# A three-branch decoder layer on eight cores: projection blocks in another order, and side branches whose waits are prepared further ahead

## The chip, the cores and the metric

The kernel runs on all 8 cores of one Trainium2 chip, and each core computes one element of the batch (2,048 tokens). The time is the device time of the slowest core in microseconds (us). Lower is better. Cores 0 to 3 are one die, cores 4 to 7 the other.

Most executions of one kernel agree within 1.5%. Some fall into a second, slower state in which the cores of one die, sometimes of both, show a lower granted TensorE clock; most of these take 6 to 14% longer, with a mean clock of 0.77 to 0.88 on a die, where the cores of fast runs have 0.89 to 0.97; a few take only up to 4% longer. Such runs are marked slow. A median, where one is given, is of all runs of that kernel, slow ones too.

Engines as the profile names them: PE is TensorE (matmuls), PEld its weight load, DVE is VectorE, ACT is ScalarE, POOL is GpSimd, SP is SyncE, which here only issues DMA transfers. `L289` is a line of the kernel file. L289 is the one helper that issues every matmul, so groups are told apart by their tiles.

## The reference, cut to what matters

```python
h = rms_norm(x, norm[l])
proj = h @ w_in[l]                                  # (B,S,IN_DIM)
(m_qk, m_v, m_o, m_z, m_i, m_f, a_cq, a_ckv, a_kr, a_z, c_q, c_z, gates) = split_cols(proj)
# A: mLSTM
qk = jax.nn.silu(causal_depthwise_conv(m_qk, conv_w[l], conv_b[l]))      # 4 taps
...
hm = mlstm_chunkwise(mq, mk, mv, ig, lf)
hm = rms_norm(hm, ...) * jax.nn.sigmoid(m_o) * jax.nn.silu(m_z)
# B: latent attention, 8 heads, causal softmax
...
ha = causal_block_attention(qa, ka, v_a) * jax.nn.silu(a_z)
# C: 4 heads over 256 memory tokens
hc = memory_attention(c_q, mkv[:, :, 0], mkv[:, :, 1]) * jax.nn.silu(c_z)
# merge
merged = g_m * (hm @ w_br_m[l]) + g_a * (ha @ w_br_a[l]) + g_c * (hc @ w_br_c[l])
x = x + merged @ w_out[l]
return rms_norm(x, final_norm)
```

## The kernel before

All instructions are written out by Python generators. A dense generator (projections, later the merge) always has TensorE work. A side generator (latent attention, then mLSTM, then memory attention) has long chains of waits. A scheduler alternates them: each `yield` tells how much TensorE time was just written, and the side generator gets a share of the dense one's.

```python
def dense_all():
    yield from p0_gen()      # norm of x, latent projections
    yield from p1_gen()      # latent up-projections, rotary
    yield from p2_gen()      # conv q/k blocks, values, output gates
    yield from p3_gen()      # memory queries and gates: cq0 cz0 cq1 cz1
    yield from d_gen()       # gates, merge, output

sides = [(mla_gen, "MLA", 0.36), (mlstm_gen, "ML", 0.36), (c_gen, "CC", 0.36)]
```

In the timelines looked at here an engine's instructions come in the order in which they were written (SyncE's in the changed kernel, 1,880 to 1,920 us: `cq`, `cz`, the store of the sums, two stores of `hc`, `rbc`, the same in every step). This matters throughout: an instruction that is ready still stands behind one that waits (in b1 below TensorE waits 56.7 us for loads that are written behind another load, in b5, where they are written ahead of it, 3.1 us).

One conv block is 16 matmuls into one bank and then this:

```python
copy("act", p[:, 3:515], bk[:, 0:512], [r_bk], [], accs=[p.r])
ts("dve", y[:], p[:, 3:515], cw[:, j, 3:4], cb[:, j:j + 1], ALU.mult, ALU.add, [p.r, r_k], [y.r])
for tap in (2, 1, 0):
    stt(y[:], p[:, tap:tap + 512], cw[:, j, tap:tap + 1], y[:], ALU.mult, ALU.add, [p.r, y.r, r_k], [y.r])
act(th[:], y[:], AF.Tanh, [y.r], [th.r], scale=0.5)
stt(o[:], th[:], 1.0, y[:], ALU.add, ALU.mult, [th.r, y.r], [o.r])
```

The mLSTM works in 16 chunks of 128 tokens. `mb` is a broadcast of the cumulative decay from device memory to all 128 partitions, `Cf` the state (f32), `Cb` its bf16 copy.

```python
B2s = tiles("mb", 2, [128, 4, 128], F32, top=True)
...
def loads1(c):                 # values, output gates, decay
    ...
    fw.dma("sp", B2s[c % 2][:], BHv[:, cols].partition_broadcast(128), reads=[dr("BH")], writes=[B2s[c % 2].r])

def P1a(c):                    # exponentials, scores, transposed keys
    act(EB[:], B2[:], AF.Exp, [B2.r], [EB.r])
    tt("dve", BM[:], B2[:], Mneg[:]..., ALU.add, [B2.r, Mneg.r], [BM.r])
    ...                        # q*EB on Pool, q.k matmuls, exp per head, product, transposes
def P1b(c, h):                 # state update of one head
    for kc in range(2):
        bu, r_bu = bub.next()                       # two banks in turn
        mm(bu, r_bu, ..., kw[:, h, kc * 128:(kc + 1) * 128], v2[:, h, 0:257], True, True, [kw.r, v2.r])
        stt(Cf[:, h, kc, 0:257], Cf[:, h, kc, 0:257], EB[:, h, 127:128], bu[:, 0:257], ALU.mult, ALU.add, ...)
    copy("act", Cb[:, h, :, 0:257], Cf[:, h, :, 0:257], [Cf.rs[h]], [Cb.rs[h]])
def P2(c, hp):                 # output of two heads, then their norm on VectorE
    ...
    rsqrt(sc[:, 8:10], sc[:, 6:8], sc[:, 10:12], sc.r)          # 14 steps on 128x2 numbers
    for e_ in range(2):
        stt(ht[:], bo[:, 0:256], sc[:, 8 + e_:9 + e_], g2[...], ALU.mult, ALU.mult, ...)

for c in range(16):
    if c + 1 < 16:
        P1a(c + 1)
    if c < 15:
        for h in range(4):
            P1b(c, h)
    hl = P2(c, 0); hl += P2(c, 1)
    if prev is not None:
        tail(c - 1, prev)
    prev = hl
    loads1(c + 2)              # the decay of chunk c+2 is asked for here
```

Memory attention runs in 16 steps (4 heads x 4 query blocks). The inverse of the softmax sums is a row of 512 numbers that must be in all 128 partitions. It goes to device memory (`RDC`) and comes back as a broadcast (`rbc`):

```python
for si, (h, qb) in enumerate(steps):
    ps = nxt
    if si + 2 < 16:
        loads(si + 2)                                  # cq, cz, three buffers each
    if si + 1 < 16:
        nxt = scores(si + 1)
    ...                                                # 8 narrow matmuls: the sums
    fw.op("dve", lambda e: e.reciprocal(out=rd[:], in_=dn[:, 0:4]), ...)
    fw.op("pe", lambda e: e.transpose(out=dn[0:4, 128:256], in_=rd[:], identity=identf[:]), ...)
    copy("dve", rt_[:], dn[0:4, 128:256], [r_dn], [rt_.r])
    fw.dma("sp", RDC_d[...], rt_[:], ...)
    fw.dma("sp", rb[:], RDC_d[h:h + 1, cols].partition_broadcast(128), ...)
    ...                                                # P.V matmuls, u = out * cz
    if fin[0] is not None:
        fin[0]()                                       # the step before: hc = u * rb, store HCT
    fin[0] = fin_
```

The softmax here doesn't subtract the row's maximum and nothing guards it: scores larger than these inputs give would overflow.

## Time and profile before

The kernel took 3,651.69 us (median of three runs, 3,631.66 to 3,657.26). The profiled execution has a span of 3,699.6 us on its slowest core, core 6. That is more than the timed runs took: in this execution cores 6 and 7 stayed some 75 us longer in the mLSTM than the other six cores, whose spans are 3,597 to 3,625 us. The page of that execution: busy time of each engine with its share of the span, then the span in 40 slices of 92.5 us, each digit the busy share of a slice in tenths (PEclk: the granted clock in tenths of full speed).

```profile
span 3699.6 us, 41439 instructions; the slowest of 8 cores (3597.0 to 3699.6 us)
...
PE 2875.4 (78%) x13618; PEld 1367.3 (37%) x13885; DVE 1295.0 (35%) x2738; ACT 761.1 (21%) x1509; POOL 341.2 (9%) x410
...
PE   3679569877779999944444446748999999999998
...
PEclk9889789989899999977777678969999999999999
```

TensorE is the busiest engine by far. Where its digits are 9 it has next to no idle time; where they are 3 to 7 it waits for something else, and that is the time a change can win. The next view gives the busy time of each engine (and the count of instructions) in five stretches of core 6, then the granted clock, the share of the DMA engines and GB/s. The stretches are: x phase and latent projections; projections with latent attention beside them; mLSTM; memory attention; merge and output.

```profile
0.00:524.00 524.00, 335.89 (x1738) 168.67 (x1768) 184.97 (x247) 158.84 (x326) 34.64 (x41) 0.86 0.45 117
524.00:1590.00 1066.00, 916.98 (x4454) 458.24 (x4541) 597.46 (x1236) 284.82 (x562) 6.87 (x13) 0.94 0.30 73
1590.00:2290.00 700.00, 311.92 (x1458) 148.89 (x1487) 243.15 (x875) 137.70 (x320) 35.79 (x32) 0.71 0.24 51
2330.00:2524.00 194.00, 116.42 (x537) 49.26 (x546) 53.11 (x102) 27.19 (x47) 11.49 (x19) 0.74 0.67 156
2524.00:3699.00 1175.00, 1154.37 (x5253) 524.20 (x5358) 208.31 (x267) 145.98 (x243) 252.41 (x306) 0.99 0.51 101
```

The mLSTM stretch is the worst: 312 of 700 us busy, at a clock of 0.71. The chain of waits inside one of its chunks (start, length, what; the line "issue" is time in which the engine waited for nothing that the profile shows) says why:

```profile
1860.98 16.63 DMA mb_122_13302<-BH
1877.71 0.70 DVE BM_127_13307 L302
1878.50 0.41 ACT DT_128_13308 L293
...
1882.80 0.49 DVE Cf_13317 L309
1883.42 4.02 PE bk L289 x10
```

The decay load is issued when the chunk before it is done, takes 16.63 us, and only then do the exponentials, the product and the state updates run, one after the other. What TensorE waited for in the mLSTM stretch (tile and engine that released it: us in total, times, longest) has the same cause in its first line, because the state update `Cf` stands behind the load:

```profile
PE bk L289 <- DVE Cf_13317 L309: 280.7, 57, 23.5
```

### The profile page before, as it was taken

How to read it: one execution, taken by the hardware profiler on the slowest of the kernel's cores; microseconds unless marked ns; L12 is line 12 of the kernel's file. 1: busy time of each engine (PE TensorE's matmuls, PEld its weight loads, DVE VectorE, ACT ScalarE, POOL GpSimd, SP SyncE). 2: the span in 40 equal slices, each digit the busy share in tenths (PEclk: the TensorE clock that was granted, in tenths of full speed). 3: DMA queues.
4: the chain of work that ended last, by engine and by line, in shares of the span. 5: the costliest groups of instructions: out<-in, count | busy, mean ns of one | idle time of the engine just before them, and what ended most of it. 6: DMA issues, size and time to landing. Idle time of an engine off the chain costs nothing.

```text
span 3699.6 us, 41439 instructions; the slowest of 8 cores (3597.0 to 3699.6 us)
## 1 busy us (share of the span) xinstructions
PE 2875.4 (78%) x13618; PEld 1367.3 (37%) x13885; DVE 1295.0 (35%) x2738; ACT 761.1 (21%) x1509; POOL 341.2 (9%) x410
## 2 busy tenths in 40 slices
PE   3679569877779999944444446748999999999998
PEld 2334334333335644422211213313444444444444
DVE  3535214567674455423333333131111111111143
ACT  4431213222222233221211112110111111111021
POOL 0002000000000000000000000002222222222100
PEclk9889789989899999977777678969999999999999
DMA  5305563232213432142323211575444564444762
GB/s 170 85 12 144 144 146 84 76 76 52 71 55 75 115 77 55 45 81 44 66 43 62 50 43 38 115 173 98 76 76 77 112 126 77 77 77 77 162 204 92
DMA packets 183522, 326.35 MB, mean 88 GB/s; under 512 B 31312, under 2 KB 123984, under 8 KB 172816
## 3 DMA queue, kind: packets, MB, share of 16 engines
q0 software_dynamic: 32832, 134.85, 21.8%
q1 hardware_dynamic: 150480, 188.83, 17.3%
q8 instruction: 115, 1.88, 0.2%
q14 instruction: 95, 0.78, 0.1%
HBM read 384.68 MB, written 73.79 MB: 124 GB/s over the span
## 4 chain that ended last, share of the span: by engine, by line
PE 60%; DMA 15%; DVE 13%; issue 6%; ACT 4%; SPq 2%; DVEq 1%; ACTq 0%; POOLq 0%
PE bk L289 59%; DMA mb_122_13302<-BH 4%; DMA mb_121_13301<-BH 3%; DVE y_100_5053 L309 2%; DVE y_101_5054 L309 2%; SPq L132 2%; DMA hb_193_19251<-HCT 1%; DVE den_80_3545 L302 1%; DMA xt_14_61<-x 1%; DMA xo_209_26268<-x 1%; DMA cq_170_18127<-CQT 1%; DVE Cf_13317 L309 1%; DVEq L71 1%; DMA RDC<-rtc_184_18141 1%; ACT DT_128_13308 L293 1%
## 5 line engine op out<-in xcount | busy, mean ns | idle before, releaser
L289 PE MATMUL bk<-hT_10_52,w_12_54 128*128 128x512 bf16 x622 | 180.2, 440 | 4.3 <-issue 2.4
L289 PE MATMUL bk<-hT_9_51,w_11_53 128*128 128x512 bf16 x657 | 173.5, 415 | 11.5 <-DMA w_11_53<-wA 7.7
L289 PE MATMUL bk<-hT_10_52,w_11_53 128*128 128x512 bf16 x653 | 168.1, 406 | 3.6 <-DVE e_3_47_3200 L309 1.9
L289 PE MATMUL bk<-hT_9_51,w_12_54 128*128 128x512 bf16 x623 | 162.2, 406 | 1.2 <-issue 0.4
L289 PE MATMUL bk<-w_11_53,hT_9_51 128*128 128x512 bf16 (+1 forms) x630 | 132.5, 363 | 19.0 <-ACT hT_9_51 L297 6.7
L289 PE MATMUL bk<-w_11_53,hT_10_52 128*128 128x512 bf16 (+1 forms) x629 | 134.6, 367 | 5.2 <-ACT hT_10_52 L297 4.8
L289 PE MATMUL bk<-hT_9_51,wg_153_18094 128*128 128x512 bf16 x503 | 116.4, 386 | 8.4 <-DMA wg_153_18094<-wGB 7.9
L289 PE MATMUL bk<-hT_9_51,wg_155_18096 128*128 128x512 bf16 x502 | 112.9, 379 | 0.5
L289 PE MATMUL bk<-hT_9_51,wg_154_18095 128*128 128x512 bf16 x502 | 112.8, 379 | 0.5
L289 PE MATMUL bk<-hT_10_52,wg_155_18096 128*128 128x512 bf16 x502 | 112.6, 379 | 0.5
L289 PE MATMUL bk<-hT_10_52,wg_154_18095 128*128 128x512 bf16 x502 | 112.4, 379 | 0.5
L289 PE MATMUL bk<-hT_10_52,wg_153_18094 128*128 128x512 bf16 x502 | 112.4, 379 | 0.5
L289 PE MATMUL bk<-w_12_54,hT_9_51 128*128 128x512 bf16 (+1 forms) x501 | 110.5, 365 | 0.7 <-issue 0.2
L289 PE MATMUL bk<-w_12_54,hT_10_52 128*128 128x512 bf16 (+1 forms) x503 | 109.0, 362 | 0.4
L309 DVE SCALAR_TENSOR_TENSOR tm_198_19257<-sg_158_18099,bk 128x512 f32<-128x512 f32 x31 | 21.3, 687 | 246.8 <-PE bk L289 246.8
L289 PEld LDWEIGHTS bk<-hT_9_51,w_11_53 128*128 128x128 bf16 x672 | 70.1, 105 | 97.1 <-issue 35.6
L309 DVE SCALAR_TENSOR_TENSOR tm_198_19257<-sg_156_18097,bk 128x512 f32<-128x512 f32 x30 | 20.6, 688 | 239.4 <-PE bk L289 239.4
L289 PEld LDWEIGHTS bk<-hT_10_52,w_12_54 128*128 128x128 bf16 x640 | 70.6, 111 | 89.6 <-issue 38.0
L289 PEld LDWEIGHTS bk<-hT_10_52,w_11_53 128*128 128x128 bf16 x672 | 69.1, 103 | 85.9 <-issue 19.7
L293 ACT ACTIVATE sg_156_18097<-bk 128x512 f32<-128x512 f32 x46 | 27.5, 597 | 342.0 <-PE bk L289 342.0
L289 PEld LDWEIGHTS bk<-hT_9_51,w_12_54 128*128 128x128 bf16 x640 | 65.6, 104 | 77.1 <-issue 17.8
L289 PEld LDWEIGHTS bk<-w_11_53,hT_9_51 128*128 128x128 bf16 x640 | 63.7, 100 | 81.3 <-issue 28.0
(607 smaller groups left out, 4813.1 us busy)
## 6 DMA issues: line engine op xcount, KB each, us to landing
w_12_54<-wA POOLq DMA_DIRECT2D x8, 2048.0 KB, 14.2
wg_153_18094<-wGB POOLq DMA_DIRECT2D x32, 512.0 KB, 5.4
wg_154_18095<-wGB POOLq DMA_DIRECT2D x32, 512.0 KB, 5.5
wg_155_18096<-wGB POOLq DMA_DIRECT2D x32, 512.0 KB, 5.5
w_11_53<-wA POOLq DMA_DIRECT2D x7, 2048.0 KB, 15.9
xt_13_60<-x SPq DMA_DIRECT2D x6, 1024.0 KB
wb_194_19253<-wGB POOLq DMA_DIRECT2D x24, 256.0 KB, 3.9
wb_195_19254<-wGB POOLq DMA_DIRECT2D x24, 256.0 KB, 3.9
```

What stands on the lines that cost most here:

```text
L71: self.eng[e].wait_ge(self._semh(key), val)
L132: ins = self.eng[q].dma_start(out=out, in_=in_)
L289: fw.op("pe", lambda e: e.matmul(bk[o] if not isinstance(o, bass.AP) else o, lhsT=lhsT, rhs=rhs, start=start, stop=stop), reads=reads, wri ...
L293: fw.op("act", lambda e: e.activation(out=out, in_=in_, func=func, **kw), reads=reads, writes=writes, accs=accs)
L302: fw.op(eng, lambda e: e.tensor_tensor(out=out, in0=in0, in1=in1, op=op), reads=reads, writes=writes, accs=accs)
L309: fw.op("dve", lambda e: e.scalar_tensor_tensor(out=out, in0=in0, scalar=sc, in1=in1, op0=op0, op1=op1), reads=reads, writes=writes, accs= ...
```

## The change

The intent is to let TensorE never stand behind a chain of small steps or a late load. The diff is 1,400 lines, most of it moved code. Its core, with cuts marked:

The norm's inverse root loses three of its fourteen steps on VectorE:

```diff
-            for _ in range(3):
+            for c in (3.0, 12.0, 768.0):
                 V(... t = y * y)
                 V(... t = t * x)
-                V(lambda e: e.tensor_scalar(out=t, in0=t, scalar1=-0.5, scalar2=1.5, op0=ALU.mult, op1=ALU.add))
-                V(lambda e: e.tensor_tensor(out=y, in0=y, in1=t, op=ALU.mult))
+                V(lambda e: e.scalar_tensor_tensor(out=y, in0=t, scalar=-c, in1=y, op0=ALU.add, op1=ALU.mult))
```

The x phase goes tile by tile: loads three tiles ahead, the memory rows as tiles 17 and 18 of the same loop, the rotary tables in single small VectorE steps between latent projections (these are cut here), weights in four DMAs with a dependency for each quarter. The projections get one list in a mixed order, in which the memory blocks stand singly among long ones:

```diff
+        MIX = ["az0", "qk0", "az1", "v0", "qk1", "me0", "oz0", "me2", "qk2", "v1", "oz1", "me1", "qk3", "me3", "v2", "oz2", "oz3"]
+        LAST = ["cq0", "cz0", "cq1", "cz1"]
...
-        sides = [(mla_gen, "MLA", 0.36), (mlstm_gen, "ML", 0.36), (c_gen, "CC", 0.36)]
+        sides = [(mla_gen, "MLA0", 0.3), (mlstm_gen, "ML", 0.45), (c_gen, "CC", 0.8)]
```

In a conv block the first tap moves from VectorE to ScalarE and the small edge copies to Pool; attention gets 0.7 of its usual share there. The causal masks of latent attention and a product of the output gates move to Pool too.

```diff
                         if tb == 0:
-                            fw.op("dve", lambda e: e.memset(p[:, 0:3], 0.0), writes=[p.r])
+                            fw.op("pool", lambda e: e.memset(p[:, 0:3], 0.0), writes=[p.r])
                         else:
-                            copy("dve", p[:, 0:3], last[0][:, 512:515], [last[0].r], [p.r])
+                            copy("pool", p[:, 0:3], last[0][:, 512:515], [last[0].r], [p.r])
                         copy("act", p[:, 3:515], bk[:, 0:512], [r_bk], [], accs=[p.r])
-                        ts("dve", y[:], p[:, 3:515], cw[:, j, 3:4], cb[:, j:j + 1], ALU.mult, ALU.add, [p.r, r_k], [y.r])
+                        act(y[:], bk[:, 0:512], AF.Identity, [r_bk, cw.r, cb.r], [y.r], scale=cw[:, j, 3:4], bias=cb[:, j:j + 1])
```

The mLSTM is cut into small slots. The decay has three buffers and is loaded three chunks ahead, its exponentials (`P1e`) are made a chunk ahead, and one norm (`P2n`) serves four heads and ends in two products on Pool:

```diff
-            B2s = tiles("mb", 2, [128, 4, 128], F32, top=True)
+            B2s = tiles("mb", 3, [128, 4, 128], F32, top=True)
...
+            def P1e(c):
+                ...
+                loads_b(c + 3)
...
+            def P2n(c):
+                hr, sc, ht, g2 = hrs[c % 2], scs[c % 2], hts[c % 2], g2s[c % 2]
+                ...
+                rsqrt(sc[:, 8:12], sc[:, 4:8], sc[:, 12:16], sc.r)
+                tt("pool", hr[:, :, 0:256], hr[:, :, 0:256], sc[:, 8:12]..., ALU.mult, [sc.r, hr.r], [hr.r])
+                tt("pool", ht[:]..., hr[:, :, 0:256], g2[:]..., ALU.mult, [hr.r, g2.r], [ht.r])
+                loads_g(c + 2)
...
+            for c in range(16):
+                P2(c, 0)
+                if c + 1 < 16:
+                    P1s(c + 1)
+                for h in range(4):
+                    if c < 15:
+                        P1b(c, h)
+                    if h == 1:
+                        ...
+                        P2(c, 1)
+                        P2n(c)
+                if c + 2 < 16:
+                    P1e(c + 2)
+                if c > 0:
+                    tail(c - 1)
+                loads_v(c + 2)
```

In memory attention the sums' transpose and store, their broadcast and the last product are each put off by a step (`dtl`, `rbl`, `fin`), with a third buffer for `u` and `rb`:

```diff
+                if dtl[0] is not None:
+                    dtl[0]()
...
-                if fin[0] is not None:
-                    fin[0]()
+                if len(fin) > 1:
+                    fin.pop(0)()
...
-                fin[0] = fin_
+                fin.append(fin_)
+                if rbl[0] is not None:
+                    rbl[0]()
+                rbl[0] = lambda ...: fw.dma("sp", rb[:], RDC_d[h:h + 1, cols].partition_broadcast(128), ...)
+                dtl[0] = dt_
```

Finally the merge asks for the branch results (`hb`, 4 MB) as soon as the mLSTM is done, while memory attention still runs.

## The prediction

> **What bounds the kernel now.** TensorE, which is not kept full. Both programs hold the same 13,755 matmuls[...]. The page: PE busy 2,875 of a 3,700 us span, mean granted clock 0.89. Table of stretches, slowest core:
> - 0 to 524 us: x, latent and memory phases. The chain of waits shows x loads (27 us first), four rotary-table blocks of 15 us on VectorE between projections, a 21 us wait for memory rows, two 16 us weight waits in the memory products.
> - 524 to 1590 us: projections with attention between. From 680 to 1100 us PE is 75% busy, VectorE 72%: each conv block of 16 matmuls holds VectorE for 0.56 + 3x0.75 us, a 0.85 us wait for tanh and 0.69 us, plus attention's 0.69 us sums: about 6.7 us a block.
> - 1590 to 2290 us: mLSTM, PE 45%, clock 0.7. A chunk takes 45 us; 13 to 18 of it is the decay load (mb from BH), issued only when the previous chunk is done, and 9 us are two runs of sixteen 0.27 us VectorE steps for the norm.
> - 2330 to 2524 us: memory attention, whose loads and reciprocal round trip (3 to 9 us) are waited for in place.
> - From 2524 us: merge and output, PE 99%, clock 1.0: 1,176 us.
>
> **The change, costed.** No PE work goes.
> 1. x phase: rotary work thinned to five VectorE steps a tile, memory rows normalized as tiles 17 and 18, weights in quarters. First gate block starts at 355 us, not 524: -170.
> 2. Mixed blocks: conv loses the 0.56 us first tap and its copies to ACT and Pool, and takes 0.7 of the attention share: about 5 us a block, still VectorE-bound; 64 blocks save 110 us. Memory products cost 27 us plus small weight waits. 524-1590 (1,066 us) becomes 950, leaving attention's last 16 us of PE work to the next stage.
> 3. mLSTM: decay loads three chunks ahead, exponentials one; one norm for four heads (14 steps, 3.8 us), then twice 2.5 us on Pool. A chunk's PE work with its projections is 12.2 us; four state products in a row use two banks behind those VectorE steps, so I expect 5 to 6 us of stall: 18 to 19 us a chunk, 300 us in all, not 700.
> 4. Memory attention with sums finished later: 6.5 us a step, not 12. 1590-2524 (934 us) becomes 560.
> 5. Merge and output: same; its 30 us data waits remain.
>
> Sum on the slowest core: 3,700 - 170 - 115 - 375 = 3,040; the decay wait, which makes cores 6 and 7 some 80 us longer, goes, so a little less.
>
> **Clock.** [...] The stretches agree (0.7 at 45% busy, 1.0 at 99%): part of the gain comes as clock.
>
> **Predicted: 3,010 us, 2,880 to 3,140 (8 in 10). Faster by over 2%: 0.97; within 2%: 0.02; slower: 0.01.**
>
> **Right or wrong shows in:** first gate block near 355 us; no mb wait in the chain; chunks of 18 to 19 us; VectorE over 80% in conv stretches; merge still 1,170 us.
>
> **What would break it:** value loads queued behind the Pool norm on the one DMA queue starving mLSTM (over 25 us a chunk); Pool masks stalling attention; or smaller stalls than I think (below 2,900).

What "The stretches agree" refers to is cut with it; its two pairs are measured (0.71 at 45% busy and 0.99 at 98% in the stretches above). 3,700 - 170 - 115 - 375 makes 3,040 us, and "a little less" took it to 3,010.

## More of the kernel before

In memory attention TensorE waits for the query loads:

```profile
PE bk L289 <- DMA cq_170_18127<-CQT: 27.3, 4, 15.6
```

## The result, and the profile after

The changed kernel took 3,184.4 us (median of four runs: 3,184.01, 3,184.78 and 3,177.92 fast, 3,499.19 slow) against 3,641.68 us of the kernel before in the same rounds. Ratios here are the mean time of one kernel's fast runs over that of the other's fast runs of the same rounds, so they are not quite the ratio of the medians: 0.8741, with a 95% interval of 0.8679 to 0.8802. The result is faster, but 174 us above the predicted 3,010 and outside the range of 2,880 to 3,140.

The page after, same views as before (slices of 79.6 us):

```profile
span 3183.0 us, 41220 instructions; the slowest of 8 cores (3143.9 to 3183.0 us)
...
PE 2821.1 (89%) x13885; PEld 1342.6 (42%) x13885; DVE 1126.1 (35%) x1994; ACT 794.6 (25%) x1593; POOL 576.2 (18%) x769
...
PE   5789988988889979987776856999999999999998
...
PEclk9899989998999999998898887999999999999999
```

And the stretches on core 7, the slowest one, in the columns used before (x phase; projections; mLSTM; memory attention; merge):

```profile
0.00:345.00 345.00, 279.80 (x1505) 135.71 (x1506) 183.50 (x261) 128.32 (x271) 36.34 (x49) 0.95 0.54 148
345.00:1388.00 1043.00, 941.46 (x4769) 472.16 (x4768) 513.11 (x915) 335.63 (x631) 164.77 (x322) 0.96 0.35 82
1410.00:1752.00 342.00, 240.46 (x1338) 126.02 (x1337) 152.19 (x420) 143.72 (x376) 108.06 (x70) 0.87 0.43 101
1816.00:2010.00 194.00, 121.15 (x559) 48.48 (x560) 53.38 (x102) 25.85 (x46) 9.97 (x17) 0.77 0.69 154
2010.00:3183.00 1173.00, 1155.84 (x5347) 523.14 (x5344) 208.30 (x267) 146.06 (x243) 253.85 (x308) 0.99 0.51 102
```

The x phase gave 179 us and the mLSTM 358 us (20.5 us a chunk, before 45; the stores of its results come every 41 us for two chunks). Some 75 us of these 358 are the extra time of cores 6 and 7 before; on the mean of the eight cores the mLSTM gave 290 us (table below). Memory attention gave nothing at all: 194 us before and after. The projections barely shrank. The decay load has left the waits. What TensorE waited for in the changed kernel's projections, 345 to 1388 us (`w` are weights, `y` and `pre` tiles of the convolution, `Pa` the probabilities of latent attention, masked on Pool):

```profile
PE bk L289 <- DMA w_11_53<-wA: 16.3, 7, 4.2
PE bk L289 <- ACT y_91_4283 L293: 11.1, 5, 8.5
PE bk L289 <- POOL Pa_70_3205 L302: 10.6, 8, 4.7
PE bk L289 <- POOL pre_89_4281 L299: 8.9, 5, 4.5
```

The same view of its mLSTM, 1410 to 1752 us:

```profile
PE bk L289 <- DVE Cf_13565 L309: 75.3, 48, 5.5
...
PE bk L289 <- DMA mv_109_13545<-MV: 6.4, 1, 6.4
```

And of its memory attention, 1816 to 2010 us:

```profile
PE bk L289 <- DMA cq_158_17636<-CQT: 25.1, 3, 11.7
PE bk L289 <- DMA cq_159_17637<-CQT: 13.8, 3, 5.5
```

The slowest core's total moves by some 20 us from run to run; the cores reach the first gate block between 341 and 351 us in this run and up to 369 us in others. The experiments are therefore also read by stage, averaged over the eight cores of the profiled execution. The marks are DMA stores that every core issues: the first latent gate (end of the x phase), the first memory query (end of the projections), the last mLSTM result, the last memory attention result.

| kernel | to first gate store | to first query store | to last mLSTM store | to last memory attention store | = time of that store |
|---|---|---|---|---|---|
| before | 504.5 | 1070.8 | 654.2 | 214.2 | 2443.8 |
| after | 346.7 | 1032.3 | 364.0 | 244.7 | 1987.6 |

The last interval includes about 60 us (before about 40 us) of dense blocks that remain after the mLSTM. From the first query load to the last store memory attention takes 170.3 us before and 170.8 after, on the mean of the cores, and from its first to its last store 133.8 and 131.8.

The sum of the prediction and the measured windows, on the slowest core:

| stretch | before | predicted | measured | off by |
|---|---|---|---|---|
| to the first gate block | 524 | 355 | 345 | -10 |
| projections and latent attention | 1066 | 950 | 1043 | +93 |
| mLSTM and memory attention | 934 | 560 | 622 | +62 |
| merge and output | 1175 | 1176 | 1173 | -3 |

These add up to +142 us over the sum of 3,040 in the prediction's text. The 30 us more that the text took off to reach 3,010 were counted twice: the sum already follows the slowest core, on which the decay wait is part of the 700 us.

### The profile page after: what moved, and what is told of

It reads as the page before. It is cut to its first block, busy times and chain, and to the rows that moved or that the text cites. A ratio compares the mean times of both kernels' runs of the same rounds, so it can differ in the third digit from the quotient of the medians.

```text
span 3183.0 us, 41220 instructions; the slowest of 8 cores (3143.9 to 3183.0 us)
## 1 busy us (share of the span) xinstructions
PE 2821.1 (89%) x13885; PEld 1342.6 (42%) x13885; DVE 1126.1 (35%) x1994; ACT 794.6 (25%) x1593; POOL 576.2 (18%) x769
## 4 chain that ended last, share of the span: by engine, by line
PE 74%; DMA 12%; DVE 6%; issue 3%; ACT 3%; POOL 1%; SPq 1%; DVEq 0%; ACTq 0%; POOLq 0%
PE bk L289 73%; DMA w_11_53<-wA 2%; DVE y_92_4284 L309 1%; DMA mv_110_13546<-MV 1%; DMA hb_157_17616<-HCT 1%; DVE y_91_4283 L309 1%; DMA xt_14_61<-x 1%; DMA cq_158_17636<-CQT 1%; SPq L132 1%; DVE Cf_13565 L309 1%; DMA cq_159_17637<-CQT 1%; DMA cq_160_17638<-CQT 1%; DMA mv_109_13545<-MV 0%; DMA cb_4277<-convb 0%; DMA RDC<-rtc_174_17652 0%
## 5 line engine op out<-in xcount | busy, mean ns | idle before, releaser
L289 PE MATMUL bk<-hT_9_51,w_11_53 128*128 128x512 bf16 x928 | 229.0, 398 | 13.5 <-DMA w_11_53<-wA 12.2
L289 PE MATMUL bk<-hT_10_52,w_11_53 128*128 128x512 bf16 x928 | 218.3, 387 | 0.6 <-ACT y_92_4284 L293 0.5
L289 PE MATMUL bk<-w_11_53,hT_9_51 128*128 128x512 bf16 (+1 forms) x640 | 149.6, 384 | 23.9 <-DMA w_11_53<-wA 17.4
L289 PEld LDWEIGHTS bk<-hT_9_51,w_11_53 128*128 128x128 bf16 x928 | 93.0, 102 | 126.0 <-issue 35.5
L289 PE MATMUL bk<-w_11_53,hT_10_52 128*128 128x512 bf16 (+1 forms) x640 | 141.8, 371 | 0.0
L289 PEld LDWEIGHTS bk<-hT_10_52,w_11_53 128*128 128x128 bf16 x928 | 91.9, 100 | 107.4 <-issue 8.7
L289 PE MATMUL bk<-hT_9_51,wg_138_17592 128*128 128x512 bf16 x512 | 119.6, 392 | 8.0 <-DMA wg_138_17592<-wGB 8.0
L289 PE MATMUL bk<-hT_9_51,wg_140_17594 128*128 128x512 bf16 x512 | 116.8, 386 | 0.0
L289 PE MATMUL bk<-hT_9_51,wg_139_17593 128*128 128x512 bf16 x512 | 116.5, 385 | 0.0
L293 ACT ACTIVATE sg_141_17595<-bk 128x512 f32<-128x512 f32 x46 | 27.5, 598 | 343.2 <-PE bk L289 343.2
L289 PE MATMUL bk<-hT_10_52,wg_138_17592 128*128 128x512 bf16 x512 | 113.1, 379 | 0.0
L289 PE MATMUL bk<-hT_10_52,wg_139_17593 128*128 128x512 bf16 x512 | 113.1, 379 | 0.0
L289 PE MATMUL bk<-hT_10_52,wg_140_17594 128*128 128x512 bf16 x512 | 113.1, 379 | 0.0
L289 PE MATMUL bk<-hT_10_52,w_12_54 128*128 128x512 bf16 x384 | 97.7, 406 | 9.7 <-ACT y_91_4283 L293 9.0
L289 PEld LDWEIGHTS bk<-w_11_53,hT_9_51 128*128 128x128 bf16 x640 | 63.9, 102 | 94.7 <-issue 36.6
L289 PE MATMUL bk<-w_12_54,hT_9_51 128*128 128x512 bf16 (+1 forms) x512 | 103.1, 353 | 0.1
L289 PE MATMUL bk<-hT_9_51,w_12_54 128*128 128x512 bf16 x384 | 99.7, 411 | 0.9 <-ACT y_91_4283 L293 0.8
L289 PE MATMUL bk<-w_12_54,hT_10_52 128*128 128x512 bf16 (+1 forms) x512 | 99.2, 344 | 0.0
L293 ACT ACTIVATE sg_143_17597<-bk 128x512 f32<-128x512 f32 x45 | 26.9, 597 | 278.7 <-PE bk L289 278.7
L289 PEld LDWEIGHTS bk<-w_11_53,hT_10_52 128*128 128x128 bf16 x640 | 63.1, 100 | 65.5 <-issue 4.4
```

What stands on the lines that cost most here:

```text
L289: fw.op("pe", lambda e: e.matmul(bk[o] if not isinstance(o, bass.AP) else o, lhsT=lhsT, rhs=rhs, start=start, stop=stop), reads=reads, wri ...
L293: fw.op("act", lambda e: e.activation(out=out, in_=in_, func=func, **kw), reads=reads, writes=writes, accs=accs)
```

## The experiments

Sixteen kernels ran. All start from the changed kernel except one, which starts from the kernel before. All gave a correct result except three that are wrong. First the measured stages of all of them, as above: the mean over the eight cores of the profiled execution, always a fast one, in us. Beside them stand the fast runs.

| run | x phase | projections | mLSTM | to last memory attention store | fast runs, us |
|---|---|---|---|---|---|
| changed kernel | 346.7 | 1032.3 | 364.0 | 244.7 | 3184.01 3184.78 3177.92 |
| a1_sums_in_place | 346.8 | 1032.3 | 371.5 | 240.4 | 3181.94 3188.47 3196.09 3185.28 |
| a2_loads_4_ahead | 347.9 | 1035.8 | 369.6 | 232.1 | 3180.53 3183.76 3168.14 |
| a3_in_place_4_ahead | 347.0 | 1033.7 | 365.1 | 224.4 | 3160.38 3169.43 3163.12 |
| a4_loads_other_queue | 347.0 | 1033.0 | 363.6 | 228.1 | 3162.7 3170.81 3171.28 |
| a6_no_round_trip | 355.4 | 1032.4 | 373.7 | 222.8 | 3199.09 3168.27 3179.62 |
| a5_no_round_trip_4_ahead | 352.3 | 1031.9 | 366.0 | 197.7 | 3151.99 3143.11 3150.66 3139.44 |
| b1_norm_last | 347.2 | 1037.4 | 360.1 | 245.4 | 3194.86 3174.05 3176.8 3180.18 |
| b6_values_first | 347.1 | 1032.9 | 361.1 | 243.3 | 3175.52 3187.53 |
| b5_norm_last_values_first | 346.4 | 1033.5 | 336.0 | 243.2 | 3151.36 3156.72 3152.58 |
| b4_grouped_order | 347.0 | 1020.3 | 364.9 | 243.8 | 3169.23 3167.83 |
| c1_masks_on_dve | 351.5 | 1014.7 | 370.2 | 247.8 | 3177.69 3189.41 |
| d2_no_taps (wrong) | 347.9 | 957.1 | 368.8 | 242.6 | 3114.88 3119.63 |
| d3_short_loads (wrong) | 352.0 | 1014.7 | 362.7 | 243.7 | 3176.51 |
| d5_three (wrong) | 350.8 | 991.1 | 370.2 | 245.7 | 3170.02 3158.94 |
| d1_all_together | 347.1 | 1003.4 | 334.7 | 199.7 | 3079.44 3093.69 3088.98 3079.32 3077.89 |
| kernel before | 504.5 | 1070.8 | 654.2 | 214.2 | see above |
| b3_before_decay_ahead (from before) | 503.9 | 1071.4 | 488.3 | 214.1 | 3478.95 3473.27 3475.88 |

A stage that an edit does not touch moves by 1 to 10 us in this table; the projections, which most edits leave alone, by 1 to 5 us. That is the resolution to read it with.

### Memory attention: loads, deferral, or the way through memory

The theory at first: in each step the query load, issued two steps ahead, still lands too late, since it stands in one queue with the stores. A rival: the inverse sums' way through device memory sets the pace, and deferring does not hide it.

**a1_sums_in_place** takes back the deferral alone (the loop body of before, with the change's first `yield`).

```diff
-            rbl, dtl = [None], [None]
+            fin = [None]
...                       # transpose, store and broadcast of the sums in the step itself
-                if len(fin) > 1:
-                    fin.pop(0)()
+                if fin[0] is not None:
+                    fin[0]()
```

> The changed kernel with one part undone: memory attention finishes each softmax sum in its own step again, as before; everything else stays. The memory attention stage took 194 us in the changed kernel (1816 to 2010 us) where I had expected 115, and 16 steps there each wait for the next score tile (cq). Theory L (score loads come too late, so the sums never were the limit): undoing costs little, total 3,170 to 3,210 us. Theory S (the deferred sums do hide their round trip, and the stage is long for another reason): undoing costs 16 times 3 to 5 us, total 3,230 to 3,270 us.

Measured: 3,186.87 us median. The stage is not longer without the deferral: 240.4 us against 244.7 (a difference within the resolution). So finishing the softmax sums a step later gained nothing, and the prediction had booked about half of the stage's time for it.

**a2_loads_4_ahead** keeps the deferral and loads the queries four steps ahead (five buffers), the gates three ahead. A first form with six buffers each found no room in memory and was not run.

```diff
-            cqs = tiles("cq", 3, [128, 2, 512], BF16, top=True)
-            czs = tiles("cz", 3, [128, 2, 512], BF16, top=True)
+            cqs = tiles("cq", 5, [128, 2, 512], BF16, top=True)
+            czs = tiles("cz", 4, [128, 2, 512], BF16, top=True)
...
-                if si + 2 < 16:
-                    loads(si + 2)
+                loads_q(si + 4)
+                loads_z(si + 3)
```

> The changed kernel with the score tiles of memory attention loaded four steps ahead instead of two (five buffers for three) and the gate tiles three ahead (four buffers for three). Theory L: the waits for cq (50 us of TensorE idle time in the stage) go, the stage shrinks from 194 to about 120 us, total 3,100 to 3,130 us. Rival, bandwidth: the stage is limited by what the DMA engines can move beside the 4 MB of branch data and gate weights, so earlier loads only shift the wait, total 3,165 to 3,190 us.

Measured: 3,182.15 us median; the stage lost 13 us, not the 50 us for which TensorE had waited for loads. TensorE's waits in this run, 1800 to 2012 us, name a new releaser in place of the old one:

```profile
PE bk L289 <- DVE rtc L299: 41.8, 16, 9.9
PE bk L289 <- DMA cq<-CQT: 11.9, 1, 11.9
```

The loads now come in time (the one wait left is the first load), and the wait reappears as `rtc`, the copy of the transposed inverse, once in every step. The first theory falls as the only cause: most of the wait moved. The total lies in the range that was written for the rival, bandwidth, but a4 below speaks against that: from 1830 to 1950 us the slowest core's DMA engines moved 168 GB/s in the changed kernel and 196 in a4, with the same loads on another queue, so they had room. The chain of waits of this run, 1900 to 1960 us (start, length, what), shows where to:

```profile
1904.64 6.00 DMA rbc<-RDC
1910.97 0.44 issue
1911.41 0.70 DVE hc L302
1912.23 0.33 SPq L132
1912.71 4.68 DMA rbc<-RDC
```

Read it as a loop of 7 to 8 us: the broadcast lands, the last product `hc` is made with it, SyncE issues the store of `hc`, and only then, 0.48 us after the start of that issue, the next broadcast. In the changed kernel the put-off broadcast of one step is written after the store of the step before, and that store waits for the earlier broadcast. Deferring moved the broadcast later in the text and, since the queue issued them in that order (in the changed kernel, 1,880 to 1,920 us, `rbc` comes 0.42 to 2.68 us after the second store of `hc`), tied each to the one before.

**a3_in_place_4_ahead** is a2 without the deferral, and **a4_loads_other_queue** is the changed kernel with the `cq` and `cz` loads issued by ScalarE's queue instead of SyncE's.

```diff
-                fw.dma("sp", cqs[i][:], CQT_d[...]
+                fw.dma("act", cqs[i][:], CQT_d[...]
```

> Both at once: sums finished in place as before, and the deeper score loads. With the two runs beside it this makes a square of two by two. Theory L with the loads out of the way: now the round trip of the sums shows, and this run is 20 to 60 us slower than the deep loads with deferred sums. If it is equal to that run within 10 us, deferring the sums is worth nothing in either setting.

> The changed kernel with the score and gate tiles of memory attention issued from the ACT engine's DMA queue instead of the SP queue, still two steps ahead. If they come late because they stand in the SP queue behind stores that wait for VectorE and for the reciprocal's round trip, the stage shrinks by 40 to 80 us as with the deeper loads, total 3,105 to 3,145 us. If two steps are simply less time than a load takes, it shrinks by less than 20 us, total 3,165 to 3,190 us.

Measured: a3 3,160 to 3,169 us and a4 3,163 to 3,171 us in their fast runs; the stage lost 20 and 17 us. a3's expectation missed: it was to be 20 to 60 us slower than a2, or equal within 10, and by the fast runs it is 13 us faster. Its stage without deferral is 8 us shorter than a2's with it (224.4 against 232.1), which fits the loop just read: in place, the broadcast is written ahead of that store. For a4 the second reading of its expectation holds, that the stage shrinks by less than 20 us. Early loads and a queue of their own are worth about the same (13 and 17 us), and in a3 and a4 too TensorE then waits for the inverse's way through memory, 39 us in each.

**a5_no_round_trip_4_ahead** takes the way through memory out. The sums are made by a matmul with a 128x128 matrix of twos, which leaves them in all partitions at once, and VectorE takes the reciprocal of the whole 128x512 tile. **a6_no_round_trip** is the same with the loads of the changed kernel. In both the deferral is gone too, so a1 and a3 are their nearest partners.

```diff
-                for b in range(4):
-                    for mt in range(2):
-                        mm(dn, r_dn, (slice(None), slice(b, b + 1)), ps[mt][:, b * 128:(b + 1) * 128], twob[:], ...)
-                fw.op("dve", lambda e: e.reciprocal(out=rd[:], in_=dn[:, 0:4]), ...)
+                for mt in range(2):
+                    mm(dn, r_dn, (slice(None), slice(None)), two128[:], ps[mt][:], mt == 0, mt == 1, ...)
+                fw.op("dve", lambda e: e.reciprocal(out=rb[:], in_=dn[:]), ...)
...                       # transpose, copy, store and broadcast are gone
```

> Theory L alone has fallen: with the score tiles four steps ahead the waits for cq went from 50 to 12 us but TensorE then waited 42 us for the reciprocal's transpose copy, because VectorE, in order, stood before it at the broadcast of the reciprocals (rbc from RDC), 4 to 7 us a step. New theory R: two chains of about 10 us a step lie side by side, the score load and the reciprocal's way through memory and back, and taking either away leaves the other; deferring the sums moved both ends of the second chain by a step and left its length. This run takes both away: score tiles four ahead, and the sums made by a matmul against a matrix of twos, which leaves them in all 128 partitions, with a reciprocal of 128x512 on VectorE in place of transpose, store and broadcast load. Theory R: the stage of 194 us shrinks to 110 to 135 us, total 3,110 to 3,135 us. Rival B (DMA bandwidth): the stage stays above 165 us, total over 3,150 us. A reciprocal of 128x512 that takes over 4 us would blur it.

> The same matmul sums without a way through memory, but the score tiles loaded two steps ahead as in the changed kernel. Theory R: the score loads alone hold the stage up, 165 us or more remain, total 3,155 to 3,185 us; waits of TensorE for cq stay at 40 us or more. If the stage shrinks as much as with both taken away, the score loads were only late because the SP queue was blocked by the broadcast's wait, and there is one chain, not two.

Measured: a5 3,150.66 us median, ratio 0.8661 (0.8626 to 0.8696); a6 fast runs 3,168 to 3,199 us, ratio 0.876 (0.8706 to 0.8815), no better in total than the changed kernel (its profiled execution was the slowest of its fast runs, with an x phase 9 us and an mLSTM 10 us longer). By stage, a6 lost 22 us and a5 lost 47 us, where early loads alone (a2) had lost 13; against the in-place a1, it is 16 us for the loads (a3), 18 for the way through memory (a6) and 43 for both (a5). Both expectations for a5 missed: the stage of 194 us became about 147, not 110 to 135 nor over 165, and the fast runs average 3,146 us, not 3,110 to 3,135. In a5 the results are stored every 6 us (in the changed kernel every 8.8 us on average). TensorE's waits of a5, 1815 to 1965 us, and then of a6, 1800 to 2012 us:

```profile
PE bk L289 <- DMA cq<-CQT: 13.2, 1, 13.2
PE bk L289 <- DVE rbc L1221: 11.5, 7, 3.5
...
PE bk L289 <- DMA cq<-CQT: 34.3, 8, 10.0
```

The other chain stands in the changed kernel's own chain of waits, 1816 to 1900 us, where one query load after another is waited for:

```profile
1859.40 9.37 DMA cq_159_17637<-CQT
...
1878.66 9.90 DMA cq_158_17636<-CQT
...
1898.87 10.51 DMA cq_160_17638<-CQT
```

So two chains held the stage up: the query load, about 10 us, and the inverse sums' way through memory, 7 to 8 us a step. With early loads TensorE waits 39 to 42 us for the way through memory; without that way it still waits 34 us for loads. Each alone is worth 13 to 22 us and both together 43 to 47, so they are neither fully side by side (then one alone would give nothing) nor quite separate. Only both together bring the step to 6 us, against the 6.5 that I had predicted for it. The cost of the new form shows too: the reciprocal of 128x512 takes 3.35 us of VectorE, five times a product of the same size (0.66 us for `uc`).

The profile shows a second fault of the term, which no run was made for. The "12 us a step" was the stage's 194 us divided by 16 steps. But on the slowest core of the changed kernel only 136 us lie between the first and the last result store; 40 us pass from the first query load to the first store, and the rest is the edge of the window. In a5 these are 87 and 37 us. The start-up stays, and 16 steps of 6.5 us did not contain it.

### mLSTM: 20.5 us a chunk, not 18 to 19

TensorE's largest wait in the changed mLSTM is for `Cf`, the state update: 75.3 us. The timeline of VectorE in one chunk of the changed kernel shows what stands ahead of the updates (start, length, engine, line, operation, tiles; the bracket tells how long the engine was idle before):

```profile
1631.28 0.16 DVE L302 TENSOR_TENSOR stm_137_13573<-hr_135_13571 128x4 f32<-128x4 f32 x1
...
1634.78 0.16 DVE L325 SCALAR_TENSOR_TENSOR stm_137_13573<-stm_137_13573 128x4 f32<-128x4 f32 x1
1634.89 1.59 DVE L309 SCALAR_TENSOR_TENSOR Cf_13565<-Cf_13565,EB_117_13553,bk 128x257 f32<-128x257 f32 x3
```

Fourteen dependent steps on 128x4 numbers, 0.27 us from start to start though each is busy only 0.16 us (the update after them, which does not need them, starts 0.11 us after the last one; what fills the time between dependent steps is not shown), stand ahead of the state updates for 3.8 us in each chunk (14 x 0.27 us). Theory: moving the norm behind the last state update frees them. Rival: the norm is only moved, and something else then takes the time.

**b1_norm_last** moves the norm behind the four heads.

```diff
                         P2(c, 1)
                         yield 0.67
-                        P2n(c)
+                P2n(c)
                 if c + 2 < 16:
```

> The changed kernel with the mLSTM norm of a chunk (14 small VectorE steps) emitted after the last two state updates of that chunk instead of before them. In the trace TensorE waits for the state update on VectorE 75 us in all, 5.5 us at a time, where the update stands behind those steps. Theory N: that wait falls to about 25 us, the mLSTM stage from 342 to about 290 us (18 us a chunk), total 3,130 to 3,150 us. Rival: a chunk is limited by VectorE and ACT work or by loads, then it stays within 10 us of 3,184 us.

Measured: fast runs 3,174 to 3,195 us, ratio 0.8741 (0.8692 to 0.8791), the same as the changed kernel. TensorE's waits in its mLSTM, 1410 to 1760 us:

```profile
PE bk L289 <- DMA mv<-MV: 56.7, 8, 25.1
PE bk L289 <- DVE Cf L309: 45.6, 46, 5.0
```

The wait for `Cf` fell by 30 us, and a wait for the value loads, 8.8 us before, rose to 56.7. The norm ends with `loads_g`, the load of the output gates, which has to wait until Pool's products have read the old ones. In the changed kernel SyncE waits 95.5 us for those products (`hmt`, 1400 to 1760 us). In b1, with the norm last, the value load follows that load 0.8 to 2.7 us later in SyncE's timeline (1450 to 1500 and 1650 to 1700 us): it now stands behind Pool's norm. This is the risk that the prediction named first under "What would break it", but it did not strike the change itself: it struck my repair.

**b5_norm_last_values_first** also writes the value load ahead of the norm; **b6_values_first** does that alone, as the control.

```diff
+                loads_v(c + 2)
+                P2n(c)
                 if c + 2 < 16:
...
-                loads_v(c + 2)
+                loads_g(c + 2)
```

> Norm last alone gained nothing: TensorE's wait for the state update fell from 75 to 46 us, but a new wait for the value loads (mv) of 57 us came, up to 25 us at once, because the load for chunk c+2 stands in the SP queue behind the gate load, which waits for Pool to finish the norm. This run keeps the norm last and issues the value load right after its buffer's last reader, ahead of the norm, and the gate load at the end. Theory Q (the queue order made the new wait): the mv wait falls under 10 us and the mLSTM stage from 342 to 280 to 300 us, total 3,125 to 3,150 us. Rival (the stage is limited by the sum of VectorE and ACT work in a chunk): within 15 us of 3,184 us.

> The other half of that square: the norm stays where the change has it, between the state updates, and only the value load is moved ahead of the norm's gate load. In the changed kernel the value loads are on the chain of waits three times (15 to 18 us each) but TensorE waits for them only 9 us. Theory Q: the 5.5 us wait for the state update stays and limits a chunk, gain 5 to 20 us, total 3,165 to 3,180 us. If the value loads were the true limit, the gain is 40 us or more.

Measured: b5 3,154.65 us median (fast runs 3,151 to 3,157), ratio 0.8627 (0.8546 to 0.8707); b6 3,175.52 and 3,187.53 us. The mLSTM stage went from 364.0 to 336.0 us in b5 and stayed at 361.2 in b6. Waits of b5, 1408 to 1725 us:

```profile
PE bk L289 <- DVE Cf L309: 64.3, 48, 8.0
PE bk L289 <- DMA mv<-MV: 3.1, 1, 3.1
```

So the place of the norm on VectorE and the order on the DMA queue are worth 28 us together and at most 4 us apart. The expectation was met for the wait for `mv` and missed for the size: it was to be 42 to 62 us off the stage and a total of 3,125 to 3,150 us. Less `Cf` wait would have been expected in b5 than 64 us; how the rest of it splits up was not tested.

Was the stall the term that the prediction had too small? Twelve chunks of the changed kernel, between two stores of its results (windows view; length, then busy time of PE):

```profile
1493.50:1736.90 243.40, 176.21 (x1001) 93.14 (x999) 115.49 (x321) 109.68 (x284) 81.30 (x54) 0.88 0.43 99
```

A chunk is 20.3 us, of which TensorE is busy 14.7 and idle 5.6; over the eight cores idle time is 5.4 to 6.0 us and busy time 14.7 to 15.1, at a mean granted clock of 0.85 to 0.88. The stall is the 5 to 6 us that I had predicted. The 12.2 us of TensorE work, an estimate whose source the prediction does not give, are what was too small, by 2.5 us. If they were meant at full clock, the granted clock makes 14 us of them (an estimate, 12.2 divided by 0.86); no run tested that. In b5 a chunk takes 18.2 to 18.8 us: with 4.3 to 5.0 us of idle time and 13.7 to 13.9 busy at 0.89 to 0.91.

**b3_before_decay_ahead** puts one part of the change into the kernel before: three buffers for the decay, loaded three chunks ahead.

```diff
-            B2s = tiles("mb", 2, [128, 4, 128], F32, top=True)
+            B2s = tiles("mb", 3, [128, 4, 128], F32, top=True)
...
                 tt("dve", BM[:], B2[:], Mneg[:]..., ALU.add, [B2.r, Mneg.r], [BM.r])
+                loads_b(c + 3)
```

> The kernel before with one part of the change alone: the decay terms (mb from BH) in three buffers instead of two, loaded three chunks ahead, each load issued as soon as its buffer's reader is emitted. Everything else as before. My reading of before: 13 to 18 us of each 45 us chunk is that load. Theory P (the load is the longest single link): the mLSTM stage of about 700 us loses 10 to 15 us a chunk, total 3,400 to 3,490 us. Rival (several links of equal length stand side by side, as in memory attention): another wait takes its place, total above 3,560 us.

Measured: 3,477.41 us median, ratio 0.9509 (0.942 to 0.9598). The mLSTM stage falls from 654 to 488 us, to 30 us a chunk. Of the stage's 290 us, 166 come from this one early load, an edit of a few lines (about 147 if cores 6 and 7 of the kernel before, which were longer, are left out of its mean). The rest of the mLSTM rework (slots, exponentials ahead, one norm) is worth the other 124.

### Projections: 1,043 us, not 950

TensorE was busy 941 of the 1,043 us. A prediction of 950 left it 9 us of idle time. Which idle time had I not counted?

The conv blocks themselves did what was predicted. Their windows, from the first to the last write of `y`: one stretch before, the sum of the four stretches after, the same sum for d2_no_taps below (length, then busy time by engine):

```profile
687.20:1132.20 445.00, 333.17 (x1431) 153.89 (x1461) 315.95 (x592) 118.76 (x240) 2.11 (x4) 0.88 0.23 60
...
sum 329.30, PE 278.01 PEld 126.47 DVE 228.86 ACT 138.31 POOL 35.64; mean PE 69.50 PEld 31.62 DVE 57.21 ACT 34.58 POOL 8.91
...
sum 255.50, PE 254.08 PEld 120.71 DVE 88.04 ACT 146.57 POOL 30.60; mean PE 63.52 PEld 30.18 DVE 22.01 ACT 36.64 POOL 7.65
```

One of the 64 blocks takes 5.1 us instead of 7.0, so the stretches are 116 us shorter, where 110 were predicted. But TensorE's busy time in them fell as well, by 55 us: with 0.7 of its share, attention has 272 weight loads in them instead of 445. That work was not gone; it had to be done elsewhere in the stage. Only 61 of the 116 us are idle time. The prediction booked all of it as a gain. VectorE is busy 67 to 72% of each stretch; the prediction's sign "VectorE over 80% in conv stretches" failed.

**b4_grouped_order** gives up the mixed order: `az0 az1 qk0..3 v0..2 me0..3 oz0..3`. The exact order of before found no room in memory and was not run.

> The changed kernel with its block order undone: gates, then the four conv blocks together, the three value blocks, the four memory products, the four output-gate blocks (the order of before cannot be had exactly, a tile finds no room then). Theory M (mixing itself matters, because VectorE-bound conv blocks and attention even out): 40 to 80 us slower, total 3,225 to 3,265 us. Theory D (the stage got shorter because each conv block holds VectorE for less, and because the memory rows were normalized early; order matters little, since a two-bank ring carries no backlog from one block into the next): within 20 us of 3,184 us.

Measured: fast runs 3,169.23 and 3,167.83 us, ratio 0.8722 (0.8673 to 0.8772). The stage is 12 us shorter than with the mixed order, not longer. Against this one other order, the mixing is worth nothing or slightly less.

**c1_masks_on_dve** gives the causal masks back to VectorE, where one takes 0.22 us (median) against 0.43 us on Pool (median; mean 0.51). The hand-over that its first theory names, from the end of ScalarE's exponential to the end of the mask on Pool, takes 0.56 us at least and 0.74 us in the median of the 128 masks of the changed kernel.

```diff
-                            tt("pool", p[:, 0:128], p[:, 0:128], maskb[:], ALU.mult, [p.r, RC], [p.r])
+                            tt("dve", p[:, 0:128], p[:, 0:128], maskb[:], ALU.mult, [p.r, RC], [p.r])
```

> The changed kernel with the causal mask of latent attention multiplied on VectorE as before, instead of on Pool. In the projection stage TensorE waits 53 us in all for work released by Pool, against 23 us for weights. Theory H (the hand-over from ACT to Pool, 0.5 to 0.75 us and two semaphores, delays the attention products): 15 to 40 us faster, total 3,145 to 3,170 us. Theory V (VectorE is the limit in the conv blocks, and 128 masks of 0.23 us put back on it cost more than they save): equal or up to 20 us slower.

Measured: fast runs 3,177.69 and 3,189.41 us, ratio 0.8709 (0.8594 to 0.8823): nothing in the total. By stage the projections are 17.5 us shorter on the mean of the cores (26 us by the two slowest cores), but the cores of that execution began the stage 5 us later and its mLSTM was 6 us longer. TensorE's waits for the masked tiles did not fall; its first line is now

```profile
PE bk L289 <- DVE Pa L302: 38.9, 35, 4.4
```

against 28.1 us in all for `Pa` on Pool in the changed kernel. What went is the wait for the convolution's edge copies `pre`, 24.8 us in the changed kernel and none here. They stand on Pool in one order with the masks (in the changed kernel a mask starts at 703.69 us and takes 0.74, a `pre` copy follows at 704.37); that this order is the reason was not tested.

After these, two questions were open: whether the rest of the idle time belonged to the conv taps or to weights, and whether the causes found would add.

**d2_no_taps** leaves the three VectorE taps out, with a wrong result.

```diff
-                        for tap in (2, 1, 0):
+                        for tap in ():
```

> Wrong result on purpose: the three VectorE taps of the convolution (0.75 us each, 64 blocks, 144 us of VectorE time) are left out, only the first tap on ScalarE stays. Theory V (the conv blocks are bound by VectorE, as predicted): the four conv stretches, 430 us in the changed kernel, fall to TensorE's busy time and the total falls by 50 to 75 us (the 73 us that TensorE stands idle in them, less the 12 us wait for the conv constants). Theory W (they are bound by TensorE's own work, and the idle time in them belongs to weights, constants and Pool masks): the total falls by less than 30 us.

Measured: 3,117.26 us median of two fast runs, 67 us below the changed kernel; ratio 0.8518 (0.8437 to 0.8599). The projections take 957.1 us, 75 less. The windows view of its slowest core (length, then busy time of PE, PEld, DVE, ACT, POOL):

```profile
351.00:1316.60 965.60, 918.33 (x4760) 468.07 (x4759) 372.54 (x724) 342.77 (x630) 159.69 (x321) 0.97 0.39 88
```

TensorE's idle time falls from 101.5 us to 47.3, and its busy time for the same work from 939 to 918 us at a slightly higher clock (0.97). So the taps, 144 us of VectorE, cost 75 us of the stage, and 74 of them lie in the conv stretches, where TensorE without taps is 99% busy at 4.0 us a block. TensorE's wait for `pre` is gone here as well. VectorE is busy only half of the stage and some 70% of the conv stretches, yet its taps are what TensorE waits behind there.

**d3_short_loads** loads only half of the weights of the four blocks that follow a memory block. A memory block has only some 7 us of TensorE work (7.4 to 8.5 us busy in the four blocks of the changed kernel), so the next weights, asked for when the block before it is done, are due at once.

```diff
-            for j in range((tot + 2047) // 2048):
+            for j in range(2 if name in ("oz0", "qk2", "qk3", "v2") else (tot + 2047) // 2048):
```

> Wrong result on purpose: of the four blocks that follow a memory block (whose products last only some 7 us), only half of the weights are loaded, the rest is what lies there. Theory W1: the four weight waits that stand in the chain of waits (18.0, 17.4, 14.3 and 9.8 us, 60 us) are lost time: the total falls by 50 to 60 us. Theory W2: attention fills most of them, and only TensorE's 23 us of waiting for weights is lost: 15 to 25 us less in the stage, hardly visible in the total.

Measured: one fast run, 3,176.51 us; the stage is 17.5 us shorter. The four loads that fill 60 us of the chain of waits are worth under a third of that. That attention's work fills the rest of the time is my reading of it; one fast run is all there is.

**d5_three** joins masks on VectorE, the short loads, and the conv constants loaded before the first gate block instead of at the first conv block (12.11 us of the chain).

> Wrong result on purpose (short loads as in the run before), with masks on VectorE and conv constants a block earlier. If the excess of the projections' stage over my prediction is these three waits, its length from the first gate store to the last query store falls from 1,041 us by 26 + 12 + 23 to about 980 us, with TensorE idle some 40 us of it and no wait for masks, constants or weights above 5 us. Rival: VectorE bounds the conv blocks and takes up the time set free: the stage stays above 1,005 us.

Measured: 3,170.02 and 3,158.94 us, ratio 0.8647 (0.8562 to 0.8733); the stage takes 991.1 us on the mean of the cores and 994.7 on the slowest, a gain of 41 us where 61 were expected; TensorE is idle 66 us of it, not 40. The expectation that no mask wait stays failed: TensorE's waits in this run still begin with

```profile
PE bk L289 <- DVE Pa L302: 44.2, 34, 4.4
```

A mask on VectorE takes half the time (0.22 us against 0.43) but shares that engine's order with the taps. Both theories had a part: shortening the three waits gained two thirds of their sum; that VectorE took the rest back is my reading of this wait and not shown by a run.

### All repairs at once

**d1_all_together** is a5, b5, c1 and the early conv constants in one kernel, with a correct result.

> Correct result. Puts together what helped alone: the memory attention without its store and broadcast and with loads four steps ahead (alone about 35 us), the mLSTM norm last with the value loads ahead of its loads (about 30 us), the latent attention's masks on VectorE (26 us in the projections' stage), and the conv constants loaded a block earlier (12 us wait). If the gains are of separate waits they add: 3,184 - 35 - 30 - 26 - 12 = 3,081 us, so 3,070 to 3,110. Rival: the gains are partly the same time (a stage that gets shorter pushes its DMA and clock cost into the next), then 3,110 to 3,150.

Measured: 3,088.98 us median; fast runs 3,077.89 to 3,093.69, ratio 0.843 (0.8377 to 0.8483) in five rounds. By stage: projections -29 us, mLSTM -29, memory attention -45 against the changed kernel. The parts had given 17.5 (c1, and the 12 us wait for the constants, never run alone), 28 (b5) and 47 (a5). The first theory holds: the gains of the three stages add. This version beats both kernels, by 15.7% and, by the ratios 0.843 and 0.8741 of different rounds, by 3.6% (3.1% by the means of the fast runs).

## Why the prediction was right or wrong

**Right: the direction and the bound.** TensorE's work was the same (13,885 weight loads on both pages), and most of the gain came from shorter idle time in the x phase and the mLSTM. A part came as clock, as predicted: in the mLSTM stretch TensorE's busy time fell from 312 to 240 us, more than its weight loads did (1,487 to 1,337), while the granted clock rose from 0.71 to 0.87.

**Right: "First gate block starts at 355 us, not 524".** It started at 345, and the merge, "still 1,170 us", took 1,173. "No mb wait in the chain" held, and b3 shows that this load alone was 166 us of the mLSTM stage.

**Wrong, and the largest part: "Memory attention with sums finished later: 6.5 us a step, not 12".** The stage took 194 us in both kernels; this term was 90 us too small. I saw one chain, the reciprocal's way through memory, and assumed that deferring it by a step would hide it. Deferring gained nothing (a1 is no slower without it). On the queue each broadcast stayed behind a store that waited for the one before, which is read from the chain of waits (in a2's, broadcasts of 6.0 and 4.7 us with the issue of a store of `hc` between them), and the query loads, issued two steps ahead, ran a second chain beside it. With early loads (a2) the way through memory is what is left; without that way (a6) it is mostly the loads. Only both out gave 6 us a step, and this took 47 us off the stage (a5). The other half of the 90 us is start-up that the division by 16 had turned into steps.

**Wrong: "524-1590 (1,066 us) becomes 950".** It took 1,043, 93 us more. Part of this is work that I had placed in the next stage: latent attention's last result was stored at 1,408 us, so the following stretch was 70 us shorter, apart from its other terms, than I had it (560 - 300 - 104 predicted for everything but mLSTM and memory attention, against 622 - 342 - 194). The size of the misplacement is worked out, not tested; with it, the projections' own error is some 23 us of the total. "About 5 us a block" was right: 5.1 us, and the three taps cost 75 us of the stage (d2). The step that failed is "64 blocks save 110 us": 55 of the 116 us by which the conv stretches shrank were attention's matmuls, placed elsewhere in the stage. So 950 us was TensorE's busy time (941) with next to nothing on top, which contradicts the "still VectorE-bound" of the same paragraph; 101.5 us of idle time were measured (149 before). Masks on Pool (17.5 us), weights after the short memory blocks (17.5 us) and the late conv constants (12 us of the chain) are waits that I had not sized. "Pool masks stalling attention" stood in the prediction as a risk, and having them on Pool did cost this.

**Wrong in size: "18 to 19 us a chunk, 300 us in all".** It was 20.5 us and 342. "5 to 6 us of stall" a chunk held (5.4 to 6.0 us of idle time). The mis-sized term is "a chunk's PE work with its projections is 12.2 us": it was 14.7 to 15.1 us, at a granted clock of 0.85 to 0.88. The named cause of the stall, state updates behind the norm's VectorE steps, is real: b5 gets 28 us back, though only when the DMA queue's order is mended as well (b1, b6), and with it the chunk takes the predicted 18 to 19 us.

**Wrong: "so a little less".** The last 30 us from 3,040 to 3,010 counted the decay wait twice.

**The clock.** That "part of the gain comes as clock" rested on two stretches of the kernel before, 0.7 at 45% busy and 1.0 at 99%. The trace of the changed kernel agrees in direction: the mLSTM stretch went from 0.71 at 45% busy to 0.87 at 70%, and memory attention, whose length did not change, from 0.74 at 60% busy to 0.77 at 62%. From 2,010 us to the end all its eight cores show a mean granted clock of 0.99 or 1.00, with TensorE over 95% busy. What sets the clock is not shown by any run.

**Masks on Pool.** A mask took 0.43 us on Pool and 0.22 us on VectorE (medians). Moving this work off the busy engine paid nothing here: the move back shortened the stage by 17.5 us, though not the total of that run (c1).

**What stays open.** In b5 TensorE still waits 64 us for the state updates. In d2, without taps, 47 us of idle time remain in the projections. Why the wait for `pre` on Pool goes both without taps (d2) and without masks on Pool (c1) was not taken apart. No run makes the start-up of memory attention shorter. The block order was tried in one grouped form only. Where the x phase's 158 us come from was read from the trace and not taken apart by runs.

## What to carry to other kernels

When a step in a loop waits, list every chain that must end before the next step, with its length. Shortening one of two chains gives only a part (here 13 to 22 us of 47), because the other then ends last, and the profile names only the one that came last. Take the start-up out before you divide a stage by its steps. When a stretch gets shorter, ask whether its idle time went or its work moved. And before trusting a predicted stage, subtract its TensorE busy time: if next to nothing is left for waits, while the text says that another engine bounds part of it, the number is wrong.
